# A second copy of x's first contraction tile at the common distance, wider first pieces in three gate units, and a later use of x1's low part

## The chip, the cores and the metric

The kernel runs on one core of a Trainium2 chip. The metric is the device time of one execution in microseconds. The kernel before ran three times without the profiler: 1003.44, 1004.01 and 1004.33 us, median 1004.01. One further execution was profiled. All times inside an execution (of instructions, blocks and waits) come from that one.

## The reference, cut to what matters

The program is a two-layer decoder trunk on one sequence of 256 tokens, width 2048. Layer one is a Mamba-2 mixer, layer two is sliding-window attention with sinks; each is followed by a residual layer norm.

```python
# layer one, 8 groups
zxbcdt = x @ w_in                      # 2048 -> 4096 (z) + 6144 (x, B, C) + 64 (dt)
...                                    # conv, silu, chunked scan, gate by silu(z), group norm
x = layernorm(alpha * x + y @ w_out)   # 4096 -> 2048

# one shared K/V, then layer two
kv   = x @ kv_w + kv_b                 # 2048 -> 512
q, g = split(x @ [w_q | w_g])          # 2048 -> 2048 each
x = layernorm(alpha * x + (attention(q, kv) * silu(g)) @ w_b)
```

All of it is float32. The change concerns only where the operands of `x @ w_in`, of `x @ w_g` and of `x @ kv_w` lie and in which order some of them are used.

## The kernel before, in words

**Products in three parts.** Each float32 operand is split into a high part in fp32r and a low part (the value less its high part, in fp32r too). A product is three matmuls into one PSUM tile: high by high, high by low, low by high; the product of the low parts is left out. `mac` (line 230, matmuls on line 232) issues the three.

**Units and halves.** Weights come from HBM as units of 128 x 2048 floats, in two halves of 128 x 1024. A half is fetched by a DMA on SP's queue into a raw tile `wr` (`load_half`, line 145), copied to the high tile `wh` by ACT (line 154), and its low part `wl` is subtracted by DVE (line 157). There are `NR` = 7 raw tiles, 4 `wh` tiles and 4 `wl` tiles, in rings: an instruction that needs a tile of a ring waits until the last reader of the tile's former contents is done. `next_unit` keeps two units loaded ahead of the one in use (`AHEAD`).

**Narrow blocks.** The input projection of layer one is done in 8 groups of 10 blocks (`group`, `block`). One block takes one unit and is `narrow` (line 327): for k = 0 to 15 three matmuls with the 128 x 128 weight tile k as the stationary operand and x's contraction tile k, 128 x 256, as the moving one, 48 matmuls in a block into one PSUM tile. After a block, `plan` and `between` insert what was noted for this place: transposes (`turn_dt` with three transposes on line 444, behind block 5 of group 0; `tr`, line 578), the small products `cb` (lines 561 and 562) and `ymm` (line 602), `norm`, and the output units of the group before (`out_units`, lines 297 to 299, at the places of `OUT_AT`). The order of PE is thus the order in which this code issues; DVE and ACT follow a scheduler, with parts of the order pinned.

**Where x lies.** x's 16 contraction tiles stay in SBUF as `xH` and `xL`, each an object of the class `Split` (line 265). `Split(name, first, at0, at1)` puts its first `first` tiles at byte `at0` modulo 256 and the rest at byte `at1` modulo 256. xH has its first tile at 0 and the others at 192; xL has its first tile at 64 and the others at 192. A unit's tiles start at byte 0 modulo 256 (`WHOLE`, line 131); buffers start at multiples of 256 bytes in the built program. In this text the **distance** of a matmul is the start of its moving tile less the start of its stationary tile, modulo 256 bytes. For a narrow block it is 0, 64, 0 in the three matmuls of k = 0, and 192 in all the others.

**First products.** The first three blocks of group 0 are computed while x arrives (`first_products`, line 336): for each k the three units take turns, one `mac` each, into three PSUM tiles. The raw tiles for these 16 arrivals are listed in `FIRST`: five are `wr` tiles.

**Gate blocks.** In layer two the 16 gate units (four blocks for each j = 0 to 3, `gate_block`, line 1006) use the same 48-matmul scheme with x1 as the moving operand. x1's tiles all lie at byte 0 modulo 256, so the break is made in the weights: `BROKEN` (line 132) puts wh's first tile at 0 and wl's first at 192, and all the others at 64. The distance is 0, 0, 64 in k = 0 and 192 in the others. `split_half` makes one ACT and one DVE instruction for each piece, so a broken unit's first half is split in 128 and 896 columns.

**K/V.** `x_stat` (line 917) multiplies with x1 as the stationary operand and 512 weight columns as the moving one, for four k to a unit: x1H by wh (line 922), x1L by wh (923), x1H by wl (924). The first unit of the first half starts right behind the transposes of x1 (`turn_x1`, line 857), whose last step is the subtraction that gives x1L on DVE (line 875).

**Queues.** SP issues nearly all DMAs, in order: the weight halves, and the loads `rb` and `el` of the decay rows. POOL issues five of the first `rb` loads and does the products `yz` (line 618).

Of the kernel before, what the change touches and what calls it, by code (L numbers as in the profile page):

```python
# [23 lines left out]
KT2 = DI // P  # L24
NHD = 64
EPS = 1e-5
NR, NH, NL = 7, 4, 4
AHEAD = 2

TD, CB0 = 5, 8  # L30

NF = 3
FIRST = [("wr", 1)] * 5 + [("e", 2)] * 2 + [("xr", 5)] + [("rb", 1)] * 2

def _order():
    steps = {0: (0, 1), 3: (1, 4), 6: (4, 7), 13: (7, 16)}
# [8 lines left out]


FILL = [6, 3]
FW = 256 + NF * 128 + 64

XK_AT = [15, 16, 17, 18]  # L50
# [29 lines left out]
def trunk(ctx: ExitStack, tc: tile.TileContext, A: dict, out: bass.AP, dbg=None):  # L80
# [17 lines left out]
    def nm(s):  # L98
        uid[0] += 1
        return f"{s}_{uid[0]}"  # L100
# [29 lines left out]

    WHOLE = [(0, 0, KT)]
    BROKEN = [[(0, 0, 1), (144, 1, KT)], [(1968, 0, 1), (16, 1, KT)]]

    def new_unit(places):
        u = Unit()
# [25 lines left out]
    def load_unit(src, places, pin=False):  # L161
        u = new_unit(places)
        raws = [load_half(u, src, c) for c in range(2)]
        for c in range(2):
            split_half(u, raws[c], c, pin, pin)
        return u

    def load_first():

        us = [new_unit([WHOLE, WHOLE]) for _ in range(NF)]  # L170
        raws = []
        for tag, n in FIRST:
            if tag == "xr":
                buf = xr_t
            elif tag == "wr":
                buf = wp.tile([P, 1024], F32, tag="wr", name=nm("first"), bufs=NR)
            else:
                buf = ap.tile([P, {"rb": 1024, "e": 1536}[tag]], F32, tag=tag, name=nm("first"), bufs=2)
# [26 lines left out]
    broken = set()  # L205
    for what, j in B_ORDER:
        if what == "g":
            broken.update(range(len(srcs), len(srcs) + 4))
        srcs += wo_srcs({"q": "wq", "g": "wg", "o": "wb"}[what], j)
    units = []  # L210
    used = [0]
# [1 line left out]
    def load_next(n, pin=False):  # L213
        for _ in range(n):
            if len(units) == 4:
                nc.sync.dma_start(cc[:], A["cc"])
            for i in [i for i, n in enumerate(XK_AT) if n == len(units)]:

                v = xr[:, i % 2, i // 2 * 1024 : i // 2 * 1024 + 1024]
                tc.keep_in_program_order(  # L220
                    nc.sync.dma_start(v, A["xk"][:, i % 2, i // 2 * 1024 : i // 2 * 1024 + 1024])
                )
            units.append(load_unit(srcs[len(units)], BROKEN if len(units) in broken else [WHOLE, WHOLE], pin))

    def next_unit():
        load_next(min(used[0] + 1 + AHEAD, len(srcs)) - len(units))
# [3 lines left out]
    def mac(ps, ah, al, bh, bl, first, last, pin=False):  # L230
        for a, b, i in ((ah, bh, 0), (ah, bl, 1), (al, bh, 2)):
            m = nc.tensor.matmul(ps, a, b, start=first and i == 0, stop=last and i == 2)  # L232
            if pin:
                tc.keep_in_program_order(m)
# [30 lines left out]
    class Split:  # L265


        def __init__(self, name, first, at0, at1):
            gap = (at1 - at0) % 256 // 4
            t = ap.tile([P, KT * S + 64], F32R, tag=name, name=name)  # L270
            a = at0 // 4
            b = a + first * S + gap
            self.first = first
            self.parts = [
                t[:, a : a + first * S].rearrange("p (k s) -> p k s", s=S),
                t[:, b : b + (KT - first) * S].rearrange("p (k s) -> p k s", s=S),
            ]
# [58 lines left out]

# [197 lines left out]

    gs = [G() for _ in range(NG)]

    def in_b(g, ps):
        gs[g].bt = ap.tile([P, S], F32, tag="bt", name=nm("bt"), bufs=1)
        conv_silu(ps, g * 6, gs[g].bt[:])
# [126 lines left out]
    def block(g, b):  # L666
        u = next_unit()
        if g == 0 and b < NF:
            ps = first_ps[b + 1]
        else:  # L670
            ps = mm_tile()
            narrow(ps, u, 0, KT)
        for fn, *a in between.pop(10 * g + b, ()):
            fn(*a)
        k = BLOCKS0[b] if g == 0 else BLOCKS[b]
        if k >= 6:
            in_z(g, k - 6, ps)
        elif k >= 2:
            in_xs(g, k - 2, ps)
        else:  # L680
            (in_b, in_c)[k](g, ps)

    def group(g):
        for b in range(10):
            with ExitStack() as behind:

                for i in ((dt_begun if b < NF else dt_ended if b < 6 else ()) if g == 0 else ()):
                    behind.enter_context(tc.issue_after(i))
                if g == 1 and b in (7, 8):
                    behind.enter_context(tc.issue_after(rooted[0]))  # L690
                block(g, b)
            with ExitStack() as behind:
                for fn, *a in plan.pop(10 * g + b, ()):
                    fn(*a)
                    if fn is norm and a == [0]:

                        behind.enter_context(tc.issue_after(rooted[0]))
            if b in OUT_AT[g]:
                out_units(g - 1, [OUT_AT[g].index(b)])
        if g == NG - 1:  # L700
            out_units(g - 1, [1])
            out_units(g - 1, [2, 3])
            for t in sorted(plan):
                for fn, *a in plan[t]:
                    fn(*a)
        elif g > 0:
            out_units(g - 1, range(len(OUT_AT[g]), 4))

    def out_units(g, nbs):
# [47 lines left out]
    between = {}  # L757
    rooted = []

    def at(t, fn, *a):  # L760
        plan.setdefault(t, []).append((fn, *a))

    at(38, rotary)
    for i, t in enumerate((13, 14, 17, 18)):
        at(t, scale_x, i)
# [148 lines left out]
        nc.vector.tensor_tensor(x1, a, b, ALU.subtract)  # L914
        nc.vector.tensor_tensor(x2, d, e, ALU.add)

    def x_stat(ps, h, u, ui, pin=False):
        for k in range(4):
            kk = ui * 4 + k
            ks = slice(k * 512, (k + 1) * 512)  # L920
            hs = slice(h * P, (h + 1) * P)
            pinned(nc.tensor.matmul(ps[:], x1H[:, kk, hs], u.h[:, ks], start=kk == 0, stop=False), pin)  # L922
            pinned(nc.tensor.matmul(ps[:], x1L[:, kk, hs], u.h[:, ks], start=False, stop=False), pin)  # L923
            pinned(nc.tensor.matmul(ps[:], x1H[:, kk, hs], u.l[:, ks], start=False, stop=kk == KT - 1), pin)  # L924


    kT = bp.tile([P, 4, S], F32, tag="kT", name="kT")
# [3 lines left out]
    for h in range(2):  # L931
        ps = mm_tile()
        for ui in range(4):
            if h == 0:
                kv_u.append(next_unit())
            x_stat(ps, h, kv_u[ui], ui, h == 0)
            if h == 0:
                for c in ((), (), (0, 1), (2, 3))[ui]:
                    turn_x1(1, c, bp, "pt", 4)
        kd = bp.tile([P, 4, 2, 64], F32, tag="qt", name=nm("kd"), bufs=2)  # L940
        nc.vector.tensor_tensor(
            kd[:, :, 0, :], ps[:, :256].rearrange("p (j d) -> p j d", j=4),
            kvb[:, :256].rearrange("p (j d) -> p j d", j=4), ALU.add,
        )
# [12 lines left out]
        later(2, ktr)  # L957
# [313 lines left out]
```

## Time and profile before

| | before |
|---|---|
| median of three runs | 1004.01 us (1003.44 to 1004.33) |
| the profiled execution's own time | 1003.76 us |
| its span | 1002.0 us, mean granted TensorE clock 0.999 |
| PE / PE weight loads busy | 994.5 / 899.6 us (99% / 90%) |
| DVE / ACT / POOL busy | 774.3 / 566.8 / 103.7 us |
| matmuls on line 232 | 1280 with each of xH·wh, xL·wh, xH·wl; 256 with each of x1H·wh, x1L·wh, x1H·wl |
| moved by DMA | 198.81 MB, 198 GB/s on average |

The span is what the profiler covers; the own time adds 1.8 us around it. Starts in rows of the trace are given in microseconds from the start of the span, to a hundredth. Matmuls are pipelined, and the duration in a row overlaps the next matmul: what a matmul costs is the distance from its start to the next one's start (its **step**). A row of windows gives a stretch, its length, the engine's busy time in it and the number of instructions that touch it.

### The profile page before, as it was taken

The page shows a single profiled execution, that of the slowest core. Times are in us where ns is not written, and L with a number is a line of the kernel's source. Part 1 is how long each engine was busy: PE and PEld are TensorE (multiplying, and loading weights), DVE is VectorE, ACT ScalarE, POOL GpSimd, SP SyncE. Part 2 cuts the span into 40 slices and gives each one's busy share as a digit, 9 for nine tenths or more (in the row PEclk, how much of TensorE's full clock was granted, in tenths as well). Part 3 has the DMA queues.
Part 4 walks back from the last instruction along what each step waited for, and adds up shares of the span by engine and source line. Part 5 has one row for each costly group of instructions (what it writes and reads, how often), then busy time and mean ns, then how long its engine had stood idle before and what let it go on. Part 6 is the DMA issues. An engine that isn't in the chain of part 4 may idle for free.

```text
span 1002.0 us, 17831 instructions
## 1 busy us (share of the span) xinstructions
PE 994.5 (99%) x7036; PEld 899.6 (90%) x7036; DVE 774.3 (77%) x1189; ACT 566.8 (57%) x987; POOL 103.7 (10%) x126
## 2 busy tenths in 40 slices
PE   9999999999999999999999999999999999999997
PEld 8999989999999998998999999888988879878975
DVE  7888897867886887786786786898778775775786
ACT  7585866647737645664663764566454543553632
POOL 0001302004003003001200300303000000000002
PEclk9999999999999999999999999999999999999999
DMA  9798477565575656656656556557655545545522
GB/s 356 261 292 298 167 269 216 188 224 175 184 244 182 216 198 197 209 200 202 200 193 212 154 190 214 165 159 250 227 189 177 163 144 180 174 145 184 178 77 84
DMA packets 58963, 198.81 MB, mean 198 GB/s; under 512 B 6560, under 2 KB 10816, under 8 KB 58624
## 3 DMA queue, kind: packets, MB, share of 16 engines
q1 hardware_dynamic: 55792, 188.20, 56.5%
q0 software_dynamic: 2336, 8.69, 2.5%
q8 instruction: 55, 0.90, 0.4%
q10 hardware_dynamic: 752, 0.79, 0.2%
q14 instruction: 28, 0.23, 0.1%
HBM read 195.43 MB, written 2.23 MB: 197 GB/s over the span
## 4 chain that ended last, share of the span: by engine, by line
PE 96%; DVE 2%; ACT 1%; issue 0%; DMA 0%; ACTq 0%; DVEq 0%
PE mm L232 52%; PE mm L297 8%; PE mm L298 8%; PE mm L299 8%; PE mm L922 3%; PE mm L923 3%; PE mm L924 3%; PE ax L602 2%; PE ax L1032 1%; PE ax L1090 1%; PE ax L578 1%; PE ax L1072 1%; PE ax L561 0%; DVE t L1170 0%; PE mm L363 0%
## 5 line engine op out<-in xcount | busy, mean ns | idle before, releaser
L157 DVE TENSOR_TENSOR wl<-wr,wh 128x1024 fp32r<-128x1024 f32 (+2 forms) x338 | 393.0, 1182 | 110.1 <-ACT wh L154 107.8
L154 ACT ACTIVATE wh<-wr 128x1024 fp32r<-128x1024 f32 (+2 forms) x338 | 333.0, 1010 | 210.5 <-issue 74.1
L232 PE MATMUL mm<-xH,wh 128*128 128x256 f32 x1280 | 355.5, 278 | 0.1
L232 PE MATMUL mm<-xL,wh 128*128 128x256 f32 x1280 | 354.6, 277 | 0.0
L232 PE MATMUL mm<-xH,wl 128*128 128x256 f32 x1280 | 354.3, 277 | 0.0
L232 PEld LDWEIGHTS mm<-xH,wh 128*128 128x128 f32 x1280 | 240.3, 188 | 2.3 <-ACT wh L187 0.8
L232 PEld LDWEIGHTS mm<-xL,wh 128*128 128x128 f32 x1280 | 240.4, 188 | 1.1
L232 PEld LDWEIGHTS mm<-xH,wl 128*128 128x128 f32 x1280 | 240.4, 188 | 0.0
L297 PE MATMUL mm<-wh,yH 128*128 128x512 f32 x256 | 101.4, 396 | 0.0
L298 PE MATMUL mm<-wh,yL 128*128 128x512 f32 x256 | 99.8, 390 | 0.0
L299 PE MATMUL mm<-wl,yH 128*128 128x512 f32 x256 | 99.7, 389 | 0.0
L618 POOL TENSOR_TENSOR yz<-yz,z 128x256 f32<-128x256 f32 x32 | 32.8, 1033 | 471.4 <-DVE yz L613 471.4
L232 PE MATMUL mm<-x1H,wh 128*128 128x256 f32 x256 | 71.9, 281 | 0.0
L467 DVE SCALAR_TENSOR_TENSOR cv<-mm,pc,cv 128x255 f32<-128x255 f32 x144 | 68.6, 477 | 3.3 <-ACT cv L465 1.9
L232 PE MATMUL mm<-x1H,wl 128*128 128x256 f32 x256 | 71.0, 277 | 0.0
L232 PE MATMUL mm<-x1L,wh 128*128 128x256 f32 x256 | 71.0, 277 | 0.0
L922 PE MATMUL mm<-wh,x1H 128*128 128x512 f32 x160 | 63.2, 395 | 0.0
L923 PE MATMUL mm<-wh,x1L 128*128 128x512 f32 x160 | 62.5, 391 | 0.2 <-DVE x1L L875 0.2
L924 PE MATMUL mm<-wl,x1H 128*128 128x512 f32 x160 | 62.4, 390 | 0.0
L297 PEld LDWEIGHTS mm<-wh,yH 128*128 128x128 f32 x256 | 48.1, 188 | 10.3 <-DVE z L554 0.9
L299 PEld LDWEIGHTS mm<-wl,yH 128*128 128x128 f32 x256 | 48.1, 188 | 10.2
L298 PEld LDWEIGHTS mm<-wh,yL 128*128 128x128 f32 x256 | 48.1, 188 | 9.0
(206 smaller groups left out, 1349.5 us busy)
## 6 DMA issues: line engine op xcount, KB each, us to landing
wr<-in_wa SPq DMA_DIRECT2D x154, 512.0 KB, 4.8
wr<-in_wo SPq DMA_DIRECT2D x64, 512.0 KB, 4.6
wr<-in_wq SPq DMA_DIRECT2D x32, 512.0 KB, 5.2
wr<-in_wg SPq DMA_DIRECT2D x32, 512.0 KB, 4.7
wr<-in_wb SPq DMA_DIRECT2D x32, 512.0 KB, 4.3
rb<-rscr SPq DMA_DIRECT2D x11, 512.0 KB, 4.0
wr<-in_wkv SPq DMA_DIRECT2D x8, 512.0 KB, 4.9
first<-in_first SPq DMA_DIRECT2D x11, 352.0 KB, 6.6
```

Of the source, the lines that this page charges most:

```text
L154: m = nc.scalar.activation(h[:, sl], v, AF.Copy)
L157: m = nc.vector.tensor_tensor(l[:, sl], v, h[:, sl].bitcast(F32), ALU.subtract)
L232: m = nc.tensor.matmul(ps, a, b, start=first and i == 0, stop=last and i == 2)
L297: pinned(nc.tensor.matmul(ps, aH[:, k, hs], u.h[:, ks], start=k == 0, stop=False), pin)
L298: pinned(nc.tensor.matmul(ps, aL[:, k, hs], u.h[:, ks], start=False, stop=False), pin)
L299: pinned(nc.tensor.matmul(ps, aH[:, k, hs], u.l[:, ks], start=False, stop=k == 3), pin)
L467: nc.vector.scalar_tensor_tensor(a[:, sft:], ps[:, : S - sft], w(3 - sft), a[:, sft:], ALU.mult, ALU.add)
L602: nc.tensor.matmul(ps[64 * r : 64 * r + 64, cols], xd[:, c, r, :], e[:, 256:] if c else e[:, :256], start=c == 0, stop=c == 1,)
L618: nc.gpsimd.tensor_tensor(v, v, st.z[i][:], ALU.mult)
L922: pinned(nc.tensor.matmul(ps[:], x1H[:, kk, hs], u.h[:, ks], start=kk == 0, stop=False), pin)
L923: pinned(nc.tensor.matmul(ps[:], x1L[:, kk, hs], u.h[:, ks], start=False, stop=False), pin)
L924: pinned(nc.tensor.matmul(ps[:], x1H[:, kk, hs], u.l[:, ks], start=False, stop=kk == KT - 1), pin)
```

## The change

Five edits:

- `Split` gets one more tile, `again`, at the same place modulo 256 as its other tiles (192). Two POOL copies, 128 x 256 each (`copy_first`), fill it for xH and xL. They are in the plan behind block 2 of group 0.
- `narrow` uses `again` for k = 0 where its argument says so. `block` says so when `steady[0]` is true: from block 5 on (`AGAIN`), a block sets it for the next one, and each visit between them (`turn_dt`, `cb`, `tr`, `ymm`, `norm`, and the output units) clears it. So 39 of the 77 narrow blocks behind the first products take `again`: blocks 7 and 8 of group 0, five in each of groups 1 to 6, and seven in group 7. In these the distance is 192 in all 48 matmuls. All are blocks whose predecessor on PE is another narrow block. The copies need 256 more columns each, and for the room `NR` goes from 7 to 6; one of the five `wr` tiles in `FIRST` becomes the `yz` tile.
- The second gate block (i = 1) of j = 0, 2 and 3 gets `BROKEN2`: two tiles apart instead of one, so that the distance is 0, 0, 64 in k = 0 and in k = 1, and 192 from k = 2 on. Its first half is split in 256 and 768 columns.
- `x_stat` with `low_last`, for the first unit of the first half alone: the eight matmuls with x1H come first, and the four with x1L last.
- The built order of PE's instructions is otherwise unchanged; ACT and DVE have three pairs of split instructions in other widths; POOL has the two copies, one behind the load of `rb` at 42.54 us and ahead of the next.

```diff
-NR, NH, NL = 7, 4, 4
+NR, NH, NL = 6, 4, 4
-FIRST = [("wr", 1)] * 5 + [("e", 2)] * 2 + [("xr", 5)] + [("rb", 1)] * 2
+FIRST = [("wr", 1)] * 4 + [("yz", 1)] + [("e", 2)] * 2 + [("xr", 5)] + [("rb", 1)] * 2
+AGAIN = 5
     BROKEN = [[(0, 0, 1), (144, 1, KT)], [(1968, 0, 1), (16, 1, KT)]]
+    BROKEN2 = [[(0, 0, 2), (272, 2, KT)], [(1840, 0, 2), (16, 2, KT)]]
...
+            places.update({len(srcs) + i: BROKEN2 if i == 1 and j != 1 else BROKEN for i in range(4)})
...
-            t = ap.tile([P, KT * S + 64], F32R, tag=name, name=name)
+            t = ap.tile([P, KT * S + 64 + S], F32R, tag=name, name=name)
             a = at0 // 4
             b = a + first * S + gap
+            self.again = t[:, b + (KT - first) * S : b + (KT - first) * S + S]
...
-    def narrow(ps, u, k0, k1, pin=False):
+    def narrow(ps, u, k0, k1, pin=False, again=False):
         for k in range(k0, k1):
             ks = slice(k * P, (k + 1) * P)
-            mac(
-                ps[:, :S], u.h[:, ks], u.l[:, ks], xH(k, k + 1)[:, 0, :], xL(k, k + 1)[:, 0, :],
-                k == 0, k == KT - 1, pin,
-            )
+            h, l = [x.again if again and k == 0 else x(k, k + 1)[:, 0, :] for x in (xH, xL)]
+            mac(ps[:, :S], u.h[:, ks], u.l[:, ks], h, l, k == 0, k == KT - 1, pin)
...
-            narrow(ps, u, 0, KT)
+            narrow(ps, u, 0, KT, False, steady[0])
+        steady[0] = 10 * g + b >= AGAIN
         for fn, *a in between.pop(10 * g + b, ()):
             fn(*a)
+            steady[0] &= fn not in visits
...
+    visits = (turn_dt, cb, tr, ymm, norm)
...
+    def copy_first():
+        for x in (xH, xL):
+            tc.keep_in_program_order(nc.gpsimd.tensor_copy(x.again, x(0, 1)[:, 0, :].bitcast(F32)))
...
+    at(NF - 1, copy_first)
...
-    def x_stat(ps, h, u, ui, pin=False):
-        for k in range(4):
+    def x_stat(ps, h, u, ui, pin=False, low_last=False):
+        todo = [(k, i) for k in range(4) for i in range(3)]
+        if low_last:
+            todo = [(k, i) for k in range(4) for i in (0, 2)] + [(k, 1) for k in range(4)]
...
-            x_stat(ps, h, kv_u[ui], ui, h == 0)
+            x_stat(ps, h, kv_u[ui], ui, h == 0, (h, ui) == (0, 0))
```

More of the change, by code (lines that the diff above doesn't have):

```diff
@@ L177, in load_first @@
             else:
-                buf = ap.tile([P, {"rb": 1024, "e": 1536}[tag]], F32, tag=tag, name=nm("first"), bufs=2)
+                w, bufs = {"rb": (1024, 2), "e": (1536, 2), "yz": (1024, 1)}[tag]
+                buf = ap.tile([P, w], F32, tag=tag, name=nm("first"), bufs=bufs)
             raws += [buf[:, i * FW : i * FW + FW] for i in range(n)]
@@ L204, in trunk @@
     srcs += wo_srcs("wo", NG - 1) + [A["wkv"][i] for i in range(4)]
-    broken = set()
+    places = {}
     for what, j in B_ORDER:
         if what == "g":
-            broken.update(range(len(srcs), len(srcs) + 4))
+            places.update({len(srcs) + i: BROKEN2 if i == 1 and j != 1 else BROKEN for i in range(4)})
         srcs += wo_srcs({"q": "wq", "g": "wg", "o": "wb"}[what], j)
@@ L222, in load_next @@
                 )
-            units.append(load_unit(srcs[len(units)], BROKEN if len(units) in broken else [WHOLE, WHOLE], pin))
+            units.append(load_unit(srcs[len(units)], places.get(len(units), [WHOLE, WHOLE]), pin))
     def next_unit():
@@ L535, in trunk @@
     gs = [G() for _ in range(NG)]
+    steady = [False]
     def in_b(g, ps):
@@ L694, in group @@
                     fn(*a)
+                    steady[0] &= fn not in visits
                     if fn is norm and a == [0]:
@@ L699, in group @@
                 out_units(g - 1, [OUT_AT[g].index(b)])
+                steady[0] = False
         if g == NG - 1:
@@ L707, in group @@
             out_units(g - 1, range(len(OUT_AT[g]), 4))
+            steady[0] = False
     def out_units(g, nbs):
@@ L915, in rope @@
         nc.vector.tensor_tensor(x2, d, e, ALU.add)
-    def x_stat(ps, h, u, ui, pin=False):
-        for k in range(4):
+    def x_stat(ps, h, u, ui, pin=False, low_last=False):
+        todo = [(k, i) for k in range(4) for i in range(3)]
+        if low_last:
+            todo = [(k, i) for k in range(4) for i in (0, 2)] + [(k, 1) for k in range(4)]
+        for k, i in todo:
             kk = ui * 4 + k
@@ L921, in x_stat @@
             hs = slice(h * P, (h + 1) * P)
-            pinned(nc.tensor.matmul(ps[:], x1H[:, kk, hs], u.h[:, ks], start=kk == 0, stop=False), pin)
-            pinned(nc.tensor.matmul(ps[:], x1L[:, kk, hs], u.h[:, ks], start=False, stop=False), pin)
-            pinned(nc.tensor.matmul(ps[:], x1H[:, kk, hs], u.l[:, ks], start=False, stop=kk == KT - 1), pin)
+            m = nc.tensor.matmul(
+                ps[:], (x1H, x1L, x1H)[i][:, kk, hs], (u.h, u.h, u.l)[i][:, ks],
+                start=(kk, i) == (0, 0), stop=kk == KT - 1 and i == 2,
+            )
+            pinned(m, pin)
     kT = bp.tile([P, 4, S], F32, tag="kT", name="kT")
```

## Prediction

> **What bounds the kernel now.** I read the page's busy times first, then the chain that ended last, then PE's waits.
>
> ```profile
> PE   994.5 (99%) x7036; PEld 899.6 (90%) x7036; DVE 774.3 (77%) x1189; ACT 566.8 (57%) x987; POOL 103.7 (10%) x126
> PE 96%; DVE 2%; ACT 1%; issue 0%; DMA 0%; ACTq 0%; DVEq 0%
> PE ax L349 <- DVE zero L338: 1.2, 1, 1.2
> PE ax L1156 <- ACT dg L1145: 0.7, 1, 0.7
> PE mm L923 <- DVE x1L L875: 0.2, 1, 0.2
> ```
>
> PE is busy 99% and makes 96% of the chain; its recorded waits sum to 2.1 us of 1002.0. So time can only come from the step of the matmuls, start to start, and from the wait on line 923. Next I looked at steps in the timeline, at three places: the first products, an ordinary block behind another block, and block 6 of group 0 with the block behind it.
>
> ```profile
> 24.26 0.28 PE L232 MATMUL mm<-xH,wh 128*128 128x256 f32 x1
> ...
> 25.28 0.28 PE L232 MATMUL mm<-xH,wh 128*128 128x256 f32 x1
> ```
>
> Here unit, weight tiles and PSUM tile change with every triple, at distance 192 throughout. Nine steps take 25.28 - 24.26 = 1.02 us: **113.3 ns** each. A change of unit at the same distance costs nothing.
>
> ```profile
> 66.10 0.28 PE L232 MATMUL mm<-xH,wh 128*128 128x256 f32 x1
> ...
> 66.82 0.28 PE L232 MATMUL mm<-xH,wh 128*128 128x256 f32 x1
> ...
> 67.16 0.28 PE L232 MATMUL mm<-xH,wh 128*128 128x256 f32 x1
> ```
>
> This block follows a block. Its first two triples take 0.72 us together, the third 0.34 again: 0.04 us lost in six steps, to a hundredth or so. They are the triple at distance 0, 64, 0 and the first one back at 192. The windows, cut at the first matmuls of blocks, give the size over a block.
>
> ```profile
> 66.10:71.57 5.47, 5.47 (x50) 1.00 0.85 297
> 43.31:49.04 5.73, 5.73 (x48) 1.00 0.87 282
> 49.04:54.52 5.48, 5.48 (x51) 1.00 1.06 304
> 717.42:723.25 5.83, 5.83 (x48) 1.00 0.77 275
> 846.82:852.65 5.83, 5.83 (x48) 1.00 0.62 198
> 922.51:928.34 5.83, 5.83 (x48) 1.00 0.53 183
> 771.28:776.93 5.65, 5.65 (x48) 1.00 0.77 281
> 729.91:735.36 5.45, 5.45 (x50) 1.00 0.28 96
> ```
>
> 48 steps of 113.3 ns are 5.44 us. The first row is that ordinary block, 0.03 above it; between 0.03 and the 0.04 of the triples I take **0.033**. The second is block 6 of group 0, 0.29 above; the third is block 7; the fourth to sixth are the second gate blocks of j = 0, 2 and 3, 0.39 above. The clock column is 1.00 in all of them, so the granted clock isn't the reason.
>
> ```profile
> 43.31 0.36 PE L232 MATMUL mm<-xH,wh 128*128 128x256 f32 x1
> 43.51 0.28 PE L232 MATMUL mm<-xL,wh 128*128 128x256 f32 x1
> ...
> 48.34 0.28 PE L232 MATMUL mm<-xH,wh 128*128 128x256 f32 x1
> ...
> 49.04 0.28 PE L232 MATMUL mm<-xH,wh 128*128 128x256 f32 x1
> ...
> 49.75 0.28 PE L232 MATMUL mm<-xH,wh 128*128 128x256 f32 x1
> ...
> 50.09 0.28 PE L232 MATMUL mm<-xH,wh 128*128 128x256 f32 x1
> ```
>
> Block 6 loses only its first step to the transposes ahead of it (0.20); its other 47 take 5.73 - 0.20 = 5.53 us, **117.7 ns** each, to the end of the block (48.34 to 49.04: six in 0.70). At 49.04 comes block 7 with the triple at 0, 64, 0; from 49.75 on its triples take 0.34. So one stream at one distance has two lasting spacings, 113.3 and 117.7 ns, and a triple at another distance can bring PE from the second to the first. That is what the first tile's odd place does: it costs 0.033 us where PE was fast already, and it saves a block where PE was slow.
>
> **The change part by part.**
>
> *The blocks with `again`* (39). For 37 of them PE was fast before (their first steps and windows are like the first row's), and the odd triple only costs. At distance 192 throughout, the block boundary should look like the first products': 37 x 0.033 = **-1.2 us** (0 if the loss belongs to the change of block itself).
>
> The other two are blocks 7 and 8 of group 0. Nothing the change does reaches the entry of block 6 (the same transposes ahead of it, the same odd triple), so I take it to be slow again. Then blocks 7 and 8 have nothing left that ends it, until the small products behind block 8. Each takes 48 x 0.1177 = 5.65 us instead of block 7's 5.48 (block 8, an ordinary block, 5.47): 0.17 + 0.18 = **+0.35 us**. If block 6 or the seam to block 7 falls into the fast spacing, this is -0.07 instead, and up to 0.29 less for block 6 itself.
>
> *Two tiles apart in three gate blocks.*
>
> ```profile
> 716.74 0.93 PE L995 MATMUL ax<-cc,qt 128*128 128x128 f32 x7
> 717.42 0.36 PE L232 MATMUL mm<-x1H,wh 128*128 128x256 f32 x1
> 717.62 0.28 PE L232 MATMUL mm<-x1L,wh 128*128 128x256 f32 x1
> ```
>
> Eight transposes and a first step of 0.20 stand ahead, and the odd triple falls into that disturbance: the block stays at 117.7 ns. The same block of j = 1 (771.28) is fast and takes 5.65. A second odd triple comes once the transposes have run through, as block 7's did. If it works, each of the three goes from 5.83 to about 5.65; the second triple's own price is that of a gate block's odd triple in fast spacing, 5.45 - 5.44 = 0.01. So 3 x 0.18 = **-0.55 us**; if not, 0 to +0.05 (three more odd steps). What follows each block is an attention product on PE, and no PE wait on it is in the list above, so the gain can pass on. The two split pieces of a half are still two instructions over the same 1024 columns: 0.
>
> *The low part later.*
>
> ```profile
> 664.24 0.50 PE L922 MATMUL mm<-wh,x1H 128*128 128x512 f32 x1
> 664.96 0.50 PE L923 MATMUL mm<-wh,x1L 128*128 128x512 f32 x1 [0.23 <-DVE x1L L875]
> 665.30 0.40 PE L924 MATMUL mm<-wl,x1H 128*128 128x512 f32 x1
> ...
> 664.30:672.10 7.80, 7.57 (x32) 5.86 (x32) 7.80 (x16) 6.77 (x13) 1.48 (x3) 1.00 0.77 244
> ...
> 670.84 1.22 DVE L157 TENSOR_TENSOR wl<-wr,wh 128x1024 fp32r<-128x1024 f32 x1
> ...
> 672.16 0.44 PE L924 MATMUL mm<-wl,x1H 128*128 128x512 f32 x1
> 672.44 0.40 PE L922 MATMUL mm<-wh,x1H 128*128 128x512 f32 x1
> ```
>
> A step of these 512-column matmuls is 0.23 us. From 664.24 to 664.96 it is 0.72, and the next 0.34: 0.60 us more than two plain steps, and eight matmuls with x1H now stand ahead of the first x1L. But the window's third busy column is DVE: 7.80 of 7.80 us. It makes the wl halves and x1L pieces for the same products, gets nothing from an earlier PE, and ends the split that began at 670.84 at 672.06. The L924 that reads it starts at 672.16, and its step is 0.28: PE is there already when the half is ready. So what PE gains at 664.5 it waits out by 672, all but those 0.05: **-0.05 us**, bounds 0 and -0.60.
>
> *Six raw tiles.*
>
> ```profile
> SPq L145 <- DVE wl L157: 643.7, 265, 10.6
> ...
> 129.50 1.07 ACT L154 ACTIVATE wh<-wr 128x1024 fp32r<-128x1024 f32 x1 [0.87 <-DMA wr<-in_wo]
> ...
> 136.13 3.49 DVE L157 TENSOR_TENSOR wl<-wr,wh 128x1024 fp32r<-128x1024 f32 x3
> ...
> 145.81 0.50 PE L297 MATMUL mm<-wh,yH 128*128 128x512 f32 x1
> ```
>
> SP already waits for DVE's splits 265 times. With one tile fewer each weight DMA leaves one split later, and with two halves to a block of 5.47 us a split comes every 2.7 us. At the tightest place I found, ACT stood 0.87 us for a DMA, so there the lateness reaches ACT and DVE: the splits to 139.62 would end near 142.3, still ahead of the product at 145.81. **0**; if the cover fails somewhere, up to 2.7 us at that place.
>
> *The two POOL copies* lie behind the `rb` load.
>
> ```profile
> 42.54 0.69 POOL L490 DMA_DIRECT2D rb<-rscr  x1 [8.34 <-ACT cv L465]
> ...
> L618 POOL TENSOR_TENSOR yz<-yz,z 128x256 f32<-128x256 f32 x32 | 32.8, 1033 | 471.4 <-DVE yz L613 471.4
> ```
>
> The nearest row is POOL's product of the same 128 x 256, 1.03 us. Two of these behind 43.23 end near 45.3, 3.7 us ahead of block 7 at 49.04, the first reader; POOL's next instruction is another `rb` load, for later decays. 0; even at twice the duration they end at 47.4.
>
> Sum: -1.2 + 0.35 - 0.55 - 0.05 = **-1.45 us** on the profiled execution's 1003.76: 1002.3. The three runs' median is 0.25 higher; I forecast **1002.4**, between the two bases (1002.3 and 1002.6).
>
> The Trainium skill, page "TensorE: Matmul & The Clock Gate", section "Step-by-step: what each phase is for", speaks against this change: it says that loading the next tile's weights takes no SBUF read bandwidth from the running matmul, each operand having a read port of its own. By that the distance between them could not matter, and the sum would lose its -1.2, +0.35 and -0.55. The trace does not agree: 0.36 against 0.34 us a triple, at a granted clock of 1.00, where only the places of the operands differ.
>
> **The rivals.**
>
> 1. *Gate blocks stay slow.* The second triple doesn't end the spacing, as the first didn't. For it: block 6 stayed slow after its odd triple, in the same situation. Against it: block 7. Then 1003.76 - 0.9 = 1002.9.
> 2. *Block 6's spacing doesn't last* into blocks 7 and 8, or block 6 is fast this time: 0.42 to 0.71 less, 1001.6 to 1001.9.
> 3. *The distance is not the cause.* The boundary of a block costs the 0.033 whatever the place (first products change units, but not after 48 matmuls into one tile). Only -0.05 is left: 1003.7.
> 4. *The wait at 664 is really saved*, DVE's later pieces being earlier than I think: 0.55 less than forecast, 1001.8.
> 5. *Slower: the slow spacing spreads.* Without the odd triple nothing in a run of blocks takes PE out of the slow spacing; if a seam between two blocks at equal distance throws it there, each block behind runs 48 x (117.7 - 113.3) = 0.21 us longer. All 37 would give +7.8 instead of -1.2: 1011. It beats the gains of 1.45 from 7 blocks on, and 0.2% (2.0 us) from 16. For it: the two spacings last, and four `again` blocks stand in a row. Against it: the first products pass dozens of changes of unit without it, and the head of each run keeps its odd triple.
>
> The sixth case, an uncovered load with six tiles, gives up to 2.7 us at a place; one such place makes 1005.1.
>
> **How the numbers follow.** Forecast 0.38; gate blocks slow 0.22; block 6 or its followers fast 0.14; wait saved 0.07; distance not the cause 0.07; slow spacing spreads 0.07; uncovered load 0.05. A measurement of this kernel can tell about 0.2%, 2.0 us, from no change; so faster means under 1002.0, and slower over 1006.0. Runs lie within 0.45 us of their median. The forecast falls under 1002.0 in a quarter to a third of its cases (0.11), rival 2 nearly always (0.13), rival 4 mostly (0.05), rival 1 hardly (0.02): 0.32 with rounding. Slower is rival 5 and the worse half of the loads: 0.10. Same: 0.58. The range from 1001.0 to 1004.6 takes in rivals 1 to 4 with the spread of runs, and leaves out rival 5 and the loads (0.12) and little below.
>
> **What would show it.** In the profile after: the block behind a block at 5.44 us in windows, all triples 0.34; blocks 7 and 8 of group 0 at 5.65; the second gate blocks of j = 0, 2, 3 at 5.65 instead of 5.83; no PE wait on x1L at 664, and PE waiting on a wl half near 672 instead; the two POOL copies over by 46. The forecast is wrong if ordinary blocks keep 5.47, if `again` blocks run at 5.65 in any group behind the first, or if PE's list of waits names a wh, wl or DMA for over 0.5 us.

## The result, and the profile after

The changed kernel takes 1002.36 us (median of 17 runs, 1002.07 to 1003.17), the kernel before 1004.09 (17 runs, 1003.44 to 1005.87). The ratio is 0.9984, 95% interval 0.9977 to 0.9991: a gain of 1.7 us, between 0.9 and 2.3. The forecast was 1002.4.

The profiled execution of the changed kernel takes 1002.19 us, its span is 1000.2; before's were 1003.76 and 1002.0. These are the lines of its page and of PE's list of waits that answer to those of before. Line 237 is now what line 232 was.

```profile
PE 992.9 (99%) x7036; PEld 898.0 (90%) x7036; DVE 775.3 (78%) x1189; ACT 566.5 (57%) x987; POOL 104.3 (10%) x128
...
PE 95%; DVE 3%; ACT 1%; issue 1%; DMA 0%; ACTq 0%; DVEq 0%
```

```profile
PE ax L354 <- DVE zero L343: 1.2, 1, 1.2
PE ax L1180 <- ACT dg L1169: 0.7, 1, 0.7
```

PE is still the bound, with the same two waits; the one on x1L is gone. PE's busy time fell by 1.6 us with the same 7036 instructions, so what changed is the step between matmuls. The windows of the blocks show where. The columns are the stretch, its length, PE's busy time and instructions on line 237, the clock, and the DMA share and rate.

```profile
43.05:48.78 5.73, 5.73 (x48) 1.00 0.95 327
48.78:54.44 5.66, 5.66 (x51) 1.00 1.03 295
54.44:60.09 5.65, 5.65 (x50) 1.00 0.92 298
66.21:71.65 5.44, 5.44 (x51) 1.00 0.83 242
716.31:721.95 5.64, 5.64 (x48) 1.00 0.81 301
770.03:775.67 5.64, 5.64 (x48) 1.00 0.77 215
845.56:851.20 5.64, 5.64 (x48) 1.00 0.64 203
921.15:926.79 5.64, 5.64 (x48) 1.00 0.57 208
```

The first three rows are blocks 6, 7 and 8 of group 0: 5.73, 5.66, 5.65, where before had 5.73, 5.48, 5.47. The fourth is the ordinary block, 5.44 for 5.47. The last four are the second gate blocks: those of j = 0, 2 and 3 took 5.83 before, and now take 5.64, as j = 1 does.

How a spacing is handed on can be read from the seam of blocks 6 and 7; block 7 begins at 48.78.

```profile
48.43 0.28 PE L237 MATMUL mm<-xH,wh 128*128 128x256 f32 x1
...
48.78 0.28 PE L237 MATMUL mm<-xH,wh 128*128 128x256 f32 x1
...
49.14 0.28 PE L237 MATMUL mm<-xH,wh 128*128 128x256 f32 x1
...
49.49 0.28 PE L237 MATMUL mm<-xH,wh 128*128 128x256 f32 x1
```

Triples of 0.35 and 0.36 us run across the seam. Unit, weights and PSUM tile change and the first k tile comes from its copy, and no step is longer or shorter for it. The ordinary block at 66.21, also behind a block, begins in the fast spacing at once:

```profile
66.21 0.28 PE L237 MATMUL mm<-xH,wh 128*128 128x256 f32 x1
...
66.55 0.28 PE L237 MATMUL mm<-xH,wh 128*128 128x256 f32 x1
...
66.89 0.28 PE L237 MATMUL mm<-xH,wh 128*128 128x256 f32 x1
```

To see where the time went I cut every profile at the same matmuls: the first of block 3, the first of K/V, the first transpose behind K/V's third unit, and the last matmul of all. The lengths are differences of starts in the trace, in us.

| | block 3 starts at | block 3 to K/V | K/V to transposes | transposes to last matmul |
|---|---|---|---|---|
| before | 26.64 | 637.59 | 8.90 | 323.30 |
| changed | 26.38 | 636.72 | 8.90 | 322.90 |
| difference | -0.26 | -0.87 | 0.00 | -0.40 |

The first column belongs to the arrival of x. In the fourteen kernels profiled here it lies between 26.21 and 27.36 whatever was edited, so its -0.26 is not put down to the change. The second column is the 37 blocks (-1.24 by the steps in the trace) and blocks 7 and 8 (+0.37). The third is the later use of x1L: nothing. The fourth is the three gate blocks (3 x -0.186 = -0.56) and +0.16 in many small differences of steps behind them and between them. About half of that, 0.08, lies in the output products of `oH` from 870.3 to 878.9; the profiles of `again_from_9` and `low_in_order` don't have it, and its cause is open. None of it is a wait in PE's list; the other profiles below that have two tiles apart in these blocks are at 322.75 to 322.83 there, so about -0.5 is usual.

### The profile page after: what moved, and what is told of

Read it like the earlier page. It is cut to its first block, busy times and chain, and to the rows that moved or that the text cites. A ratio compares the mean times of both kernels' runs of the same rounds, so it can differ in the third digit from the quotient of the medians.

```text
span 1000.2 us, 17832 instructions
## 1 busy us (share of the span) xinstructions
PE 992.9 (99%) x7036; PEld 898.0 (90%) x7036; DVE 775.3 (78%) x1189; ACT 566.5 (57%) x987; POOL 104.3 (10%) x128
## 4 chain that ended last, share of the span: by engine, by line
PE 95%; DVE 3%; ACT 1%; issue 1%; DMA 0%; ACTq 0%; DVEq 0%
PE mm L237 52%; PE mm L944 10%; PE mm L304 8%; PE mm L305 8%; PE mm L306 8%; PE ax L609 2%; PE ax L1056 1%; PE ax L1114 1%; PE ax L585 1%; PE ax L1096 1%; DVE wl L160 1%; PE ax L568 0%; DVE t L1194 0%; DVE st L847 0%; PE mm L368 0%
## 5 line engine op out<-in xcount | busy, mean ns | idle before, releaser
L311 DVE SCALAR_TENSOR_TENSOR xr<-mm,r,xr 128x512 f32<-128x512 f32 x64 | 47.1, 745 | 12.0 <-PE mm L306 7.6
```

The lines of the kernel that those rows point to most:

```text
L311: nc.vector.scalar_tensor_tensor(v, ps, rms[:, h : h + 1], v, ALU.mult, ALU.add)
```

## The experiments

The theory: at one distance PE keeps one of two spacings, 113.3 or 117.7 ns, and hands it on over block boundaries; an odd triple (one at another distance) in an undisturbed stream costs 0.033 us in the fast spacing and ends the slow one; an odd triple that falls into a disturbance does not end it reliably. The rivals are in the expectations. All edits are made to the changed kernel. Where nothing else is said, a kernel ran once, under the profiler. What it shows is read from windows and from lengths as in the table, since times of one kernel spread over 1.1 us (1002.07 to 1003.17 for the changed one).

**1. Blocks 7 and 8 keep the odd place** (`again_from_9`).

```diff
-AGAIN = 5
+AGAIN = 8
```

> Blocks 7 and 8 of group 0 keep x's first tile at its odd place; all else as in the changed kernel. Theory (block 6's slow spacing of 117.7 ns lasts until a triple at another distance ends it): block 7 begins in the slow spacing and leaves it in its first two triples, 5.47 to 5.48 us from first matmul to the next block's first; block 8 5.48; against 5.65 and 5.65 in the changed kernel. The span is 0.35 us shorter. Rival (in the changed kernel these two blocks are slow for another reason, such as the POOL copies that lie in SBUF beside them or the wr ring of six): both stay near 5.65.

Blocks 6, 7 and 8 in its windows:

```profile
43.30:49.04 5.74, 5.74 (x49) 1.00 0.96 332
49.04:54.50 5.46, 5.46 (x50) 1.00 1.02 322
54.50:59.98 5.48, 5.48 (x50) 1.00 0.87 240
```

Block 6 is slow, and block 7's odd triple ends it. Block 3 to K/V is 636.36, 0.36 less than the changed kernel. In the changed kernel these two blocks lose by `again`.

**2. One tile apart in the gate blocks** (`one_tile_gates`).

```diff
-BROKEN2 if i == 1 and j != 1 else BROKEN
+BROKEN
```

> The second gate block of j = 0, 2 and 3 has one tile apart again, as before. Theory (the second odd triple is what ends the slow spacing): each of the three is at 5.83 us again instead of 5.64, the span 0.55 us longer. Rival (the earlier start of these blocks, or the state in which PE comes to them, made them fast, not the second tile): they stay at 5.64 to 5.65.

The second gate blocks of j = 0, 1 and 3 (j = 2 is like 0):

```profile
716.88:722.70 5.82, 5.82 (x48) 1.00 0.89 331
770.73:776.38 5.65, 5.65 (x48) 1.00 0.70 225
...
921.96:927.79 5.83, 5.83 (x48) 1.00 0.58 186
```

All three are slow again, and the last stretch takes 323.32 for 322.90. The block of j = 1, with one tile apart in every version so far, is fast. The gain is the second tile's. It could come from the second triple itself or from the other widths of the split pieces that go with it. The steps speak for the triple: in the changed kernel's three blocks the first step is 0.20 us and no later one inside the block is over 0.121, so PE waits for no piece there; the steps fall to 0.113 behind the second triple.

**3. No block reads the copy** (`no_again`).

```diff
-        steady[0] = 10 * g + b >= AGAIN
+        steady[0] = False
```

> All blocks read x's first tile at its odd place; the copies are made and not read, the ring has six raw tiles, the gate blocks and the low part are as changed. Theory: each of the 37 ordinary blocks is at 5.47 us again (+1.2), blocks 7 and 8 of group 0 at 5.47 (-0.35): the span is 0.85 us longer than the changed kernel's, and 0.6 shorter than before's. Rival (the 37 blocks got shorter by something else, such as the order of DMAs with six raw tiles): they stay at 5.44.

Block 8 of group 0 (block 7 is like it), then the two ordinary blocks behind each other in group 1:

```profile
55.23:60.70 5.47, 5.47 (x50) 1.00 0.89 301
66.82:72.29 5.47, 5.47 (x50) 1.00 0.88 285
72.29:77.77 5.48, 5.48 (x50) 1.00 1.01 357
```

Block 3 to K/V takes 637.59, as before to the hundredth. This kernel has the ring of six raw tiles, the `yz` tile in `FIRST` and the POOL copies: together they cost nothing in these 637 us. Its own time of 1003.97 came with block 3 at 27.36, the latest of all; its other three stretches sum to 969.31, against 969.79 of before and 968.52 of the changed kernel.

**4. x1L in the old order** (`low_in_order`).

```diff
-x_stat(ps, h, kv_u[ui], ui, h == 0, (h, ui) == (0, 0))
+x_stat(ps, h, kv_u[ui], ui, h == 0)
```

> The first K/V unit uses x1L in the old order; all else as changed. Theory (PE gains 0.5 us ahead of the first x1L and waits it out for DVE's split of the third unit by about 8 us later): the wait on x1L near 663 is back (0.2 us in the list of waits, a step of 0.7), the wait on wl near 671 is gone, and the transposes of x1 behind the third unit start as late after the first K/V matmul's x1L subtraction as in the changed kernel, within 0.1 us. Rival (the gain is kept): everything behind 672 is 0.4 to 0.6 us later against the x1L subtraction on DVE.

The wait on x1L is back, and K/V to transposes is 8.90, the same. The wait near 671 is not quite gone: a step of 0.34 instead of 0.23 is left there. Where the gain goes in the changed kernel is in its timeline; the second row of the second view is a weight load.

```profile
669.70 1.22 DVE L160 TENSOR_TENSOR wl<-wr,wh 128x1024 fp32r<-128x1024 f32 x1
```

```profile
670.44 0.39 PE L944 MATMUL mm<-wh,x1L 128*128 128x512 f32 x1
670.97 0.19 PEld L944 LDWEIGHTS mm<-wl,x1H 128*128 128x128 f32 x1 [0.57 <-DVE wl L160]
670.97 0.50 PE L944 MATMUL mm<-wl,x1H 128*128 128x512 f32 x1
671.31 0.40 PE L944 MATMUL mm<-wh,x1H 128*128 128x512 f32 x1
```

The split ends at 670.92. PE's step ahead of the matmul that reads it is 0.53 instead of 0.23, and the next is 0.34: PE came early and waited. PE's own list of waits doesn't name this, since the idle time lies under the modelled end of the matmul ahead; the step shows it, and so does the weight load, which waited 0.57 us for the same split.

**5. A DVE piece on POOL, with either order** (`low_last_pool`, `in_order_pool`). If DVE's chain sets the time, a lighter DVE should let the gain through.

```diff
-                nc.vector.tensor_scalar(v, v, mv[:, 0:1], rs[:], ALU.subtract, ALU.mult)
+                ops = nc.gpsimd if (h, c) == (1, 2) else nc.vector
+                ops.tensor_scalar(v, v, mv[:, 0:1], rs[:], ALU.subtract, ALU.mult)
```

> The changed kernel with one of the two DVE pieces of the second half's layer norm (0.5 us near 668.6) moved to POOL, which is idle there; x1L still comes last. Theory (DVE's chain of splits sets when PE goes on near 671): the split of the third unit's second half ends 0.4 us earlier, PE's wait for it (0.3 us) goes, and the transposes of x1 behind the third unit come 0.3 to 0.45 us earlier after the first K/V matmul. Rival (the gain is lost to something else): they come as late as in the changed kernel.

> The same piece on POOL, with x1L used in the old order. Theory: PE waits 0.5 us for x1L near 663 as before, arrives at the third unit's second half no earlier than the split, and the transposes behind the third unit come at most 0.1 us earlier than in the changed kernel: the later use of x1L is worth 0.3 us or more here, where it was worth nothing with DVE full. Rival: the same as with x1L last.

K/V to transposes: 8.79 with x1L last, 8.82 in order. The order was worth 0.03, not 0.3: a miss. The timeline of `low_last_pool` says why (the piece left on DVE, the piece on POOL); behind it stands the row of the changed kernel, where DVE does both.

```profile
668.77 0.87 DVE L875 TENSOR_SCALAR xr<-xr,mv,rs 128x512 f32<-128x512 f32 x1
...
668.55 2.14 POOL L875 TENSOR_SCALAR xr<-xr,mv,rs 128x512 f32<-128x512 f32 x1 [34.89 <-ACT rs L854]
```

```profile
668.14 1.00 DVE L874 TENSOR_SCALAR xr<-xr,mv,rs 128x512 f32<-128x512 f32 x2
```

DVE's two pieces took 1.00 together. With one of them on POOL the other alone took 0.87: DVE was freed of 0.13 us only, and the transposes came 0.11 earlier. So the runs agree with DVE as the limit, and were too small to show the rest.

**6. The piece left out** (`low_last_less`).

```diff
-                nc.vector.tensor_scalar(v, v, mv[:, 0:1], rs[:], ALU.subtract, ALU.mult)
+                if (h, c) != (1, 2):
+                    nc.vector.tensor_scalar(v, v, mv[:, 0:1], rs[:], ALU.subtract, ALU.mult)
```

> The changed kernel (x1L last) with one of the two DVE pieces of the second half's layer norm left out (columns 1024 to 1535 of the second 128 tokens stay uncentred; 0.5 us near 668.6). The run with this piece on POOL freed DVE of 0.12 us only, since its neighbour on DVE went from 0.54 to 0.87 us beside POOL's. Theory (DVE's chain sets when PE goes on behind 670): the split of the third unit's second half ends about 0.45 us earlier, and the transposes of x1 behind the third unit begin 8.45 to 8.5 us after the first K/V matmul, against 8.90 in the changed kernel and 8.82 with the old order and POOL, where PE no longer waited for the split. Rival (the gain is lost elsewhere): 8.8 or more.

```profile
663.19 0.50 PE L945 MATMUL mm<-wh,x1H 128*128 128x512 f32 x1
...
669.33 1.22 DVE L160 TENSOR_TENSOR wl<-wr,wh 128x1024 fp32r<-128x1024 f32 x1
...
671.69 1.03 PE L882 MATMUL ax<-cc,xr 128*128 128x128 f32 x8
```

The split ends 670.55 - 663.19 = 7.36 us after the first K/V matmul, where the changed kernel has 670.92 - 663.10 = 7.82, and the transposes come at 671.69 - 663.19 = 8.50. Of DVE's 0.46 us, 0.40 arrives behind the third unit. The old order was not run with the piece left out; in `in_order_pool`, where PE no longer waited for the split (its steps there are 0.22 and 0.23), it stood at 8.82. I take that as the bound that the wait on x1L sets; by it the later use would be worth 0.32 here, which no pair of runs shows directly.

**7. No odd triple in any narrow block** (`no_odd_tile`). x's first tile lies at 192 like the rest, for all blocks.

```diff
-    xH = Split("xH", 1, 0, 192)
-    xL = Split("xL", 1, 64, 192)
+    xH = Split("xH", 1, 192, 192)
+    xL = Split("xL", 1, 192, 192)
```

> x's first tile lies at 192 like all others, in all blocks; the odd triple is nowhere in the narrow blocks. Theory (the odd triple releases PE from the slow spacing that an interruption leaves, and the blocks behind keep what the first of a run has): at least some of the blocks behind transposes or small products run at 117.7 ns from their first to their last matmul, 5.65 us and more, with the blocks behind them up to the next interruption; each costs 0.2 us, so that the span is longer than the changed kernel's by 0.2 us for each slow block less 0.03 for each of the 38 that keep an odd triple there. Rival (slow spacing in block 6 of group 0 is a single accident, and the odd triple is only a cost): all blocks behind interruptions reach 113.3 ns by themselves, blocks 6 to 8 of group 0 apart, and the span is up to 1.2 us shorter.

Its time is 1015.2 us, and block 3 to K/V 648.89. The first two windows are blocks 6 and 7 of group 0 (block 8 is like 7), the last two blocks 0 and 1 of group 3:

```profile
43.85:49.40 5.55, 5.55 (x49) 1.00 0.95 325
49.40:54.84 5.44, 5.44 (x51) 1.00 1.06 304
...
236.01:241.66 5.65, 5.65 (x48) 1.00 0.50 153
241.66:247.31 5.65, 5.65 (x50) 1.00 0.33 103
```

63 of the 77 narrow blocks are 0.19 to 0.22 us longer than in the changed kernel: all 25 behind an output unit, the 30 that stand behind one of these in an unbroken row of blocks, and eight more. Those are the block behind the small products `ymm` in group 1 with the two that follow it, and the blocks behind the eight transposes `tr` in groups 2 to 6. That is 12.7 us in sum. The spacing can outlast such transposes: these five come from a slow block and stay slow (5.74), while block 2 of group 1, behind the same eight transposes but coming from a fast block, stays fast (5.53). The group norm's small products (`norm`) and `cb` ahead of block 5 of group 7 do end it: that block comes from a slow one and is fast (5.54). The run also tells the place from the copy: blocks 3 to 5 of group 0, which read no copy in either kernel, take 5.44 here and 5.47 in the changed kernel. Against the theory's plain form, some heads of runs do without an odd triple: block 6 of group 0 is fast here, and slow wherever the odd triple stands in it alone. So the odd triple can lock as well as free, and the spacing at an entry seems to depend on the pattern of steps there and on the state that PE comes with; no run here varies that pattern by itself.

**8. A second odd triple in block 6** (`two_odd_block6`, at k = 1; `odd_at_k8`, at k = 8). Only the places of this one unit's weight tiles change; the pieces are read by `u.tile`.

```diff
-    places = {}
+    places = {6: [[(0, 0, 1), (176, 1, 2), (320, 2, KT)], [(0, 0, 1), (160, 1, 2), (320, 2, KT)]]}
...
+    places = {6: [[(0, 0, 8), (1072, 8, 9), (1216, 9, KT)], [(0, 0, 8), (1056, 8, 9), (1216, 9, KT)]]}
```

> The unit of block 6 of group 0 has its second tile shifted in wh and wl, so that the block has an odd triple at k = 1 too (distance 0, 0, 64 there), as the gate blocks have; blocks 7 and 8 use the copy, as in the changed kernel. Two more split instructions on ACT and DVE. Theory (the first odd triple falls into the disturbance by the three transposes, a second one ends the slow spacing): block 6 takes 5.48 to 5.50 us instead of 5.73, and blocks 7 and 8 are at 5.44 without a triple of their own, since the fast spacing is handed on like the slow one; together about 0.65 us less span than the changed kernel. Rival (block 6 is slow for what happens beside it, such as ACT, DVE and POOL at work in the same stretch): block 6 stays at 5.73 and blocks 7 and 8 at 5.65.

> In block 6 of group 0 the second odd triple stands at k = 8 (distance 0, 0, 64 there), far behind the transposes and with the unit's second half split long before; two more split instructions. Blocks 7 and 8 on the copy. Theory (an odd triple in an undisturbed stream ends the slow spacing, and the spacing is handed on from block to block): steps of 117.7 ns to k = 7, then 113.3 from about k = 9 on, block 6 near 5.65 us, blocks 7 and 8 at 5.44. Rival (in the run with the second odd triple at k = 1 it was PE's short wait on a split, not the triple, that ended the slow spacing): 117.7 ns to the end of block 8, 5.73, 5.65 and 5.65.

The first gave 5.65, 5.44 and 5.44 for blocks 6 to 8. But the smaller split pieces came so late that PE stood once inside the block: a step of 193 ns at k = 2, with steps near 118 ahead and 113 soon behind it. So triple and wait can't be told apart there, which is why the second was run. Its windows, and its timeline around k = 8 at 46.73:

```profile
43.82:49.46 5.64, 5.64 (x48) 1.00 0.95 328
49.46:54.90 5.44, 5.44 (x50) 1.00 1.08 307
54.90:60.34 5.44, 5.44 (x50) 1.00 0.91 312
```

```profile
46.38 0.28 PE L239 MATMUL mm<-xH,wh 128*128 128x256 f32 x1
...
46.73 0.28 PE L239 MATMUL mm<-xH,wh 128*128 128x256 f32 x1
...
47.08 0.28 PE L239 MATMUL mm<-xH,wh 128*128 128x256 f32 x1
...
47.42 0.28 PE L239 MATMUL mm<-xH,wh 128*128 128x256 f32 x1
```

The triple of k = 7 takes 0.35, that of k = 8 0.35, that of k = 9 0.34, and so it stays to the end of block 8. An odd triple in mid-stream ends the slow spacing at once, with no wait near it: every step around it is between 0.113 and 0.121 us.

**9. Gate blocks without an odd triple** (`gates_even`). All tiles of the gate units at 64, distance 192 throughout.

```diff
+    EVEN = [[(16, 0, KT)], [(16, 0, KT)]]
...
-BROKEN2 if i == 1 and j != 1 else BROKEN for i in range(4)
+EVEN for i in range(4)
```

> All 16 gate units lie at byte 64 modulo 256 throughout, so that the distance is 192 in all their matmuls and there is no odd triple in a gate block. Theory: the gate blocks that follow K/V-like products of 512 columns (the first of j = 0, 2 and 3) go slow, as the narrow blocks behind output units did without the odd triple: 5.65 us instead of 5.46. The blocks behind another gate block keep what that one had. For the second blocks, which follow eight transposes, the theory names no side; if they are fast without any odd triple (5.64 us), the odd one-tile place is itself what locks them, as in block 6 of group 0. Rival (the odd triple has no part in the gate blocks): all as in the changed kernel.

The four blocks of j = 0:

```profile
710.12:715.78 5.66, 5.66 (x48) 1.00 0.89 306
716.57:722.39 5.82, 5.82 (x48) 1.00 0.55 191
723.49:729.24 5.75, 5.75 (x48) 1.00 0.46 154
729.24:734.90 5.66, 5.66 (x50) 1.00 0.28 93
```

All four of j = 0 are slow (5.46, 5.64, 5.58 and 5.45 with their odd triples), and so are the first three of j = 2 and 3 and the fourth of j = 2; all of j = 1 are fast (as long as in the changed kernel, to 0.02). The first blocks follow 512-column products of K/V's kind, as the theory said. The second blocks of j = 0, 2 and 3 are slow with no odd triple and with one, and fast with two: there one odd tile is too little, and it is not what makes them slow.

**10. A better version** (`again_from_block5`): the copies ahead of the first `rb` load on POOL, and blocks 5 and 6 of group 0 on the copy too.

```diff
-AGAIN = 5
+AGAIN = 4
...
-    visits = (turn_dt, cb, tr, ymm, norm)
+    visits = (cb, tr, ymm, norm)
...
+    for x in (xH, xL):
+        tc.keep_in_program_order(nc.gpsimd.tensor_copy(x.again, x(0, 1)[:, 0, :].bitcast(F32)))
     load_decay(0, 0)
...
-    at(NF - 1, copy_first)
```

> The changed kernel with the two POOL copies ahead of the first rb load (near 33 us instead of 43), and blocks 5 and 6 of group 0 on the copy as well; the three transposes ahead of block 6 no longer bring the odd triple back. In the run without any odd triple block 6 left the slow spacing by itself (its first steps 202, 116, 117, 120, 116, 114 ns). Theory (block 6 locks slow because the odd triple falls into the disturbance by the transposes): block 5 takes 5.44 us, block 6 5.54, blocks 7 and 8 5.44; together 0.65 us less than the changed kernel, so 1001.7 us against 1002.4. Rival (block 6 is slow in any kernel in which POOL copies or loads differ): 1002.3 or more.

Blocks 6 to 8 (block 5 took 5.44):

```profile
43.41:48.96 5.55, 5.55 (x49) 1.00 0.93 312
48.96:54.40 5.44, 5.44 (x51) 1.00 1.01 285
54.40:59.84 5.44, 5.44 (x50) 1.00 0.91 269
```

Block 3 to K/V takes 636.08, 0.64 less than the changed kernel: the stages came out as expected. Its median is 1002.16 us (11 runs, 1001.44 to 1003.03), the ratio to the kernel before 0.998, interval 0.9971 to 0.9989. That is 0.2 under the changed kernel's median, from other runs, where 0.7 was expected. A difference of 0.6 us is too small to be told from these times, and only the trace shows it.

## Why the prediction was right

- **Ordinary blocks, -1.2.** 37 blocks of 5.44 for 5.47; by steps in the trace 33 or 34 ns each, -1.24. The step that could fail, that a block boundary at equal distance costs nothing, held at every seam. Rival 3 falls: with the copies made and not read, the loss was back (experiment 3), and with the first tile itself at 192, blocks that read no copy gained it too (experiment 7). The forecast's own row of 0.36 against 0.34 us a triple could not show this, since a block boundary stood there as well.
- **Blocks 7 and 8, +0.35.** +0.37, since block 6 entered slow again. Experiment 1 takes it back by the odd triple alone. Rival 2 did not occur in the changed kernel.
- **Gate blocks, -0.55.** -0.56 at the blocks. The last stretch as a whole gained 0.40 in the profiled execution and about 0.5 in the other profiles; the rest was lost in small steps elsewhere in it. Experiment 2 shows that the second tile did it, so rival 1 falls. My reason for it, that the first triple is spent in the disturbance, is only half shown: with no odd triple these blocks lock too (experiment 9), but block 6 of group 0 is fast without one (experiments 7 and 10).
- **The low part later, -0.05.** 0.00. Of PE's 0.5 us, 0.42 was waited out at the split of the third unit's second half, as worked out, and the rest ahead, at the start of the second unit (steps of 0.25 and 0.34 near 666); experiment 6 gets 0.40 through by taking work from DVE. Rival 4 falls for the kernel as it is.
- **Six raw tiles and POOL, 0.** 0 over 637 us (experiment 3). The arrival of x, where the list of raw tiles changed too, is not covered by this: its one profile before (26.64) lies among the thirteen behind the change (26.21 to 27.36). The two copies took 0.41 and 1.42 us, not 1.03 each:

```profile
42.81 0.41 POOL L776 CAST xH<-xH 128x256 fp32r<-128x256 f32 x1
43.15 1.42 POOL L776 CAST xL<-xL 128x256 fp32r<-128x256 f32 x1
```

  They ended at 44.57, 4.2 us ahead of block 7.
- **Rival 5, the spreading slow spacing.** No block on the copy went slow of itself. But its mechanism is real: taking the odd triple from the heads of runs as well makes 63 blocks slow and costs 13 us (experiment 7). Its price in the forecast was 1.2 us too high: 0.21 us a block is counted from the fast spacing, so 37 slow blocks give -1.2 + 7.8 = +6.6, near 1010 and not 1011. The change is safe because it keeps the odd place at every head; blocks 7 and 8 are the one run where the head did not settle.
- **The sum.** -1.24 + 0.37 - 0.50 = -1.4 by the stages (-1.3 in the profiled pair), -1.57 between the two profiled executions (of which 0.26 is x's arrival), -1.73 between medians with an interval from -0.9 to -2.3. The forecast's -1.45 is the stages' sum; the other 0.3 of the medians has no stage that is shown to give it, and x's arrival alone varies by over 1 us. That the median came so near 1002.4 is partly luck.
- **The spread of runs.** The forecast said that runs lie within 0.45 us of their median. That misread the three runs before, of which the lowest lies 0.57 under it; the changed kernel's highest lies 0.81 over its own. The chances of "faster" and "slower" rest on a spread that is too small.

The Trainium skill's rule that the forecast weighed ("TensorE: Matmul & The Clock Gate", "Step-by-step: what each phase is for") is that loading the next weights takes no read bandwidth from the running matmul. That rule gives no reason for what this trace shows, 12.7 us in the blocks for the place of x's first tile, at a clock of 1.00; whether reads collide here at all, no run shows.

What stays open is why there are two spacings, and which patterns of steps lead to which. The runs show that the relative place of the two operands matters, whether x's tile is moved or the weights', and that the state lasts. Only the distances 0, 64 and 192 occur in these blocks, so the rule for other distances is open too. A conflict between the reads of the moving and of the next stationary tile would fit, and no run here measures it.

## What to carry to other kernels

Where one engine is busy 99% of the time, compare the steps of equal instructions, not their durations: two blocks with the same work and 4% between their steps can differ in nothing but where operands lie and what PE did just before. A fix that resets such a state belongs where the state can go wrong; elsewhere it is a cost, and a place where the state stays wrong loses by the fix's removal. And a wait that is taken away on PE is a gain only if the engine that feeds the next product is not full until then.

## What the runs showed that I had not expected

- The slow spacing is the usual one behind 512-column products at distance 192: each narrow block behind an output unit goes to 117.7 ns without an odd triple (experiment 7), and each gate block behind K/V's kind (experiment 9).
- An odd triple can also lock: block 6 of group 0 takes 5.73 with one in its first triple, 5.55 with none, and 5.64 with a second one at k = 8.
- A 128 x 512 piece that took DVE about 0.5 us took 0.87 while POOL worked on the piece beside it, and POOL 2.14 (experiment 5).
- Of two equal POOL copies the first took 0.41 us, the second 1.42. In the thirteen kernels that have them they take 0.39 to 1.47. Every copy that began 0.2 us or more into one of DVE's splits ended only behind that split (here the split runs from 42.82 to 44.31, the copy from 43.15 to 44.57); the copies that did not took 0.39 to 0.42.
